# Row variances of an 8192 x 8192 matrix: 64 KiB pieces on one queue, a quarter of each row summed on ScalarE, last row in shrinking pieces

## The chip, the cores and the metric

The kernel runs on one core of a Trainium2 chip. The metric is the time of one execution on the device in microseconds (us), the median of several runs. The profile kept for each kernel is that of one of these executions; its span is about 1.8 us shorter than the time (653.6 against 655.4 us for the kernel before); it is counted from the first instruction of the program. Every run quoted here was at the full granted clock.

## The reference

```python
x = np.random.randn(8192, 8192).astype(np.float32)   # 268.44 MB
out = np.var(x, axis=1)                               # 8192 variances
```

Every element must be loaded once and used once, so there are two candidates for the bound: the loads, and the engine that reduces.

## The kernel before

A tile is 128 rows, one row of 8192 values (32 KiB) per partition. It is loaded as two halves of 2 MiB, one from SyncE's and one from ScalarE's queue; a half is 16 KiB per partition. VectorE computes count, mean and squared deviation of each stretch of 512 columns (`bn_stats`), and one `bn_aggr` joins the 16 stretches of the row. At the end TensorE turns the 64 columns of variances into rows, and one transfer writes them.

```python
data = ctx.enter_context(tc.tile_pool(name="data", bufs=4))
CH = 2; spc = nsub // CH; LOOK = 3                  # nsub = 16
def issue_dma(t):
    xt = data.tile([P, nsub, FMAX], mybir.dt.float32)
    for c in range(CH):
        lo = c * spc; hi = lo + spc
        dma_eng[c % 2].dma_start(out=xt[:, lo:hi, :], in_=x_t[t, :, lo:hi, :])
    ...
def compute(t):
    ...
    for j in range(nsub):
        nc.vector.bn_stats(out=st[:, j, :], in_=xt[:, j, :])
    mv = stats.tile([P, nc.vector.BN_AGGR_DIM], mybir.dt.float32)
    nc.vector.bn_aggr(out=mv, in_=st)
    nc.gpsimd.tensor_copy(out=var_all[:, t : t + 1], in_=mv[:, 1:2])
...
nc.tensor.transpose(vp, var_all, ident)             # after the loop
nc.scalar.copy(vs, vp)
nc.sync.dma_start(out=out_t, in_=vs)
```

## Time and profile before

| | before |
|---|---|
| time, median of 4 runs | 655.37 us (655.24 to 655.69) |
| span of the profiled run | 653.6 us |
| VectorE busy | 636.2 us (97%) |
| pace of the loads in the middle | 428 GB/s |

Loads are carried by 16 transfer engines, piece by piece; such a piece, here 16 KiB, is called a packet below. The page of the kernel before: busy time by engine, the two loading queues with the instruction queue (packets, MB, share of the 16 transfer engines' time), the chain of work that ended last, and VectorE's groups (busy us, mean ns of one, idle before them and what ended it).

```profile
PE 0.4 (0%) x1; PEld 0.1 (0%) x1; DVE 636.2 (97%) x1088; ACT 1.5 (0%) x2; POOL 12.4 (2%) x70
...
q1 hardware_dynamic: 9296, 134.25, 48.4%
q10 hardware_dynamic: 9216, 134.22, 48.2%
q14 instruction: 12, 0.10, 0.0%
...
DVE 88%; DMA 6%; issue 5%; SPq 0%; PE 0%; ACT 0%; POOLq 0%; POOL 0%
...
L61 DVE BATCH_NORM_STATS2 st<-xt 128x6 f32<-128x512 f32 x1024 | 610.1, 673 | 13.6 <-DMA xt<-in_x_dram 13.6
L63 DVE BATCH_NORM_AGGREGATE mv<-st 128x2 f32<-128x96 f32 x64 | 36.4, 570 | 0.1
```

VectorE looks like the bound: it waits 13.6 us in all, nearly all of it for the first tile. But the two loading queues together were also active for 96.6% of the transfer engines' time. The next view tells the two apart. It is the kernel before in chosen stretches of the span (us): length, busy time of each engine with its number of instructions, granted clock, share of the transfer engines' time, GB/s.

```profile
200.00:300.00 100.00, 0.00 (x0) 0.00 (x0) 100.00 (x172) 0.00 (x0) 1.83 (x10) 1.00 1.01 428
620.00:625.00 5.00, 0.00 (x0) 0.00 (x0) 5.00 (x9) 0.00 (x0) 0.18 (x1) 1.00 1.01 429
625.00:630.00 5.00, 0.00 (x0) 0.00 (x0) 5.00 (x10) 0.00 (x0) 0.00 (x0) 1.00 0.80 341
630.00:635.00 5.00, 0.00 (x0) 0.00 (x0) 5.00 (x9) 0.00 (x0) 0.18 (x1) 1.00 0.06 26
635.00:640.00 5.00, 0.00 (x0) 0.00 (x0) 5.00 (x10) 0.00 (x0) 0.00 (x0) 1.00 0.03 13
```

In the middle the transfer engines are never idle (share 1.01) and carry 428 GB/s, a little more than VectorE consumes: its period is 9.934 us per tile of 4.194 MB, 422 GB/s. Both are saturated and almost equally fast. The last lines matter as much: most transfer engines finish at about 630 us, but 26 GB/s remain until 635 and 13 in the stretch after it. 428/16 is 26.8, so this is one engine of the 16, some 8 us late. A tile is complete only when its last engine has delivered, so this engine decides when VectorE may start. The end of VectorE's timeline before (start, length, instructions):

```profile
630.32 9.53 DVE L61 BATCH_NORM_STATS2 st<-xt 128x6 f32<-128x512 f32 x16
639.77 0.57 DVE L63 BATCH_NORM_AGGREGATE mv<-st 128x2 f32<-128x96 f32 x1
640.26 8.93 DVE L61 BATCH_NORM_STATS2 st<-xt 128x6 f32<-128x512 f32 x15
649.29 0.59 DVE L63 BATCH_NORM_AGGREGATE mv<-st 128x2 f32<-128x96 f32 x1
```

The landing records (each transfer engine reports when its part of a load has arrived) show the last tile complete at 638.46 us, 7.8 us after its second latest engine, and VectorE began it at 640.26. Relieving VectorE alone can hardly gain anything.

### The profile page before, as it was taken

Reading aid. Unit: us, or ns where it says so; the run is one execution under the profiler, and the core shown is the slowest. Engines: PE = TensorE matmul, PEld = TensorE weight load, DVE = VectorE, ACT = ScalarE, POOL = GpSimd, SP = SyncE. Lnnn points to the kernel's source line nnn. Section 1 sums busy time; section 2 is a strip of 40 time slices with the busy share of each in tenths; the row PEclk is TensorE's granted clock in tenths of the full one; section 3 lists DMA queues with packets and bytes.
Section 4 is the critical chain, followed back from the end, with each engine's and each line's share of the span. In section 5 each row is a group of like instructions: output and inputs, shape, how many; then the busy total and the mean of one; then the engine's idle time right before and its main releaser. Section 6 shows DMA issues by size and latency. Waiting matters only on the chain.

```text
span 653.6 us, 1512 instructions
## 1 busy us (share of the span) xinstructions
PE 0.4 (0%) x1; PEld 0.1 (0%) x1; DVE 636.2 (97%) x1088; ACT 1.5 (0%) x2; POOL 12.4 (2%) x70
## 2 busy tenths in 40 slices
PE   0000000000000000000000000000000000000000
PEld 0000000000000000000000000000000000000000
DVE  2999999999999999999999999999999999999997
ACT  0000000000000000000000000000000000000000
POOL 0000000000000000000000000000000000000000
DMA  8999999999999999999999999999999999999950
GB/s 369 433 430 425 427 432 428 425 431 428 427 428 430 427 427 430 427 427 428 428 426 431 427 429 427 426 429 428 428 427 430 427 428 429 429 425 430 429 222 2
DMA packets 18524, 268.57 MB, mean 411 GB/s; under 512 B 2064, under 2 KB 2128, under 8 KB 2128
## 3 DMA queue, kind: packets, MB, share of 16 engines
q1 hardware_dynamic: 9296, 134.25, 48.4%
q10 hardware_dynamic: 9216, 134.22, 48.2%
q14 instruction: 12, 0.10, 0.0%
HBM read 268.44 MB, written 0.03 MB: 411 GB/s over the span
## 4 chain that ended last, share of the span: by engine, by line
DVE 88%; DMA 6%; issue 5%; SPq 0%; PE 0%; ACT 0%; POOLq 0%; POOL 0%
DVE st L61 82%; DMA xt<-in_x_dram 6%; DVE mv L63 5%; SPq L54 0%; PE vp L74 0%; ACT vs L76 0%; POOLq L103 0%; POOL var_all L64 0%
## 5 line engine op out<-in xcount | busy, mean ns | idle before, releaser
L61 DVE BATCH_NORM_STATS2 st<-xt 128x6 f32<-128x512 f32 x1024 | 610.1, 673 | 13.6 <-DMA xt<-in_x_dram 13.6
L63 DVE BATCH_NORM_AGGREGATE mv<-st 128x2 f32<-128x96 f32 x64 | 36.4, 570 | 0.1
L64 POOL COPY var_all<-mv 128x1 f32<-128x1 f32 x64 | 11.7, 183 | 637.1 <-DVE mv L63 637.1
L76 ACT ACT_TABLE_LOAD x1 | 1.3, 1283 | 609.9 <-DMA xt<-in_x_dram 609.9
L74 PE MATMUL vp<-ident,var_all 128*64 128x128 f32 x1 | 0.4, 421 | 650.2 <-POOL var_all L64 650.2
L76 ACT COPY vs<-vp 64x128 f32<-64x128 f32 x1 | 0.3, 258 | 39.5 <-PE vp L74 39.5
masks.py:199 POOL TENSOR_SCALAR_AFFINE_SELECT ident<-ident 128x128 f32<-128x128 f32 x1 | 0.3, 292 | 0.1
L74 PEld LDWEIGHTS vp<-ident,var_all 128*64 128x64 f32 x1 | 0.1, 128 | 650.2 <-POOL var_all L64 650.2
masks.py:197 POOL MEMSET ident<- 128x128 f32 x1 | 0.2, 204 | 0.3 <-POOLq L92 0.3
L92 POOL MEMSET const-float32-0.0<- 128x1 f32 x1 | 0.1, 98 | 0.2 <-issue 0.2
L92 POOL MEMSET const-bfloat16-1.0<- 128x1 bf16 x1 | 0.1, 101 | 0.0
L92 POOL MEMSET const-uint8-127<- 128x1 uint8 x1 | 0.1, 101 | 0.0
L92 POOL MEMSET const-float32-1.0<- 128x1 f32 x1 | 0.1, 98 | 0.0
## 6 DMA issues: line engine op xcount, KB each, us to landing
xt<-in_x_dram ACTq DMA_DIRECT2D x64, 2048.0 KB, 29.1
xt<-in_x_dram SPq DMA_DIRECT2D x64, 2048.0 KB, 28.9
out_dram<-vs SPq DMA_DIRECT2D x1, 32.0 KB, 1.8
```

Source lines behind the costliest of these rows:

```text
L61: nc.vector.bn_stats(out=st[:, j, :], in_=xt[:, j, :])
L63: nc.vector.bn_aggr(out=mv, in_=st)
L64: nc.gpsimd.tensor_copy(out=var_all[:, t : t + 1], in_=mv[:, 1:2])
L74: nc.tensor.transpose(vp, var_all, ident)
L76: nc.scalar.copy(vs, vp)
L92: nc = _bacc.Bacc("TRN2", target_bir_lowering=False, num_devices=1)
```

## The change

The intent: take work off VectorE, so that the loads alone bound the kernel; make the loads' pieces larger; and let the last data arrive in shrinking pieces, so that little work is left behind it.

- A tile is now 256 rows: two adjacent rows per partition, 64 KiB contiguous in memory, loaded by one 8 MiB transfer on SyncE's queue, with three buffers. There are 32 tiles.
- VectorE does 12 of the 16 stretches of a row. ScalarE sums the other 2048 columns, shifted by a mean from the first stretch, and sums their squares; GpSimd turns the two sums into one more entry for the aggregate.
- The last tile comes as one row and then 4096, 2048, 1024, 512, 256, 256 columns of the other row, which VectorE does alone. Its variances are written by a transfer of their own.

```diff
-    data = ctx.enter_context(tc.tile_pool(name="data", bufs=4))
+    data = ctx.enter_context(tc.tile_pool(name="data", bufs=3))
...
+    x_t = x.rearrange("(t p j) f -> t p (j f)", p=P, j=J)          # J = 2
...
+    def row_stats(xt, j):
+        for c in range(DC):                                        # DC = 12
+            bn(st, c, xt[:, o + c * F : o + (c + 1) * F])
+        k = st[:, 1:2]
+        src = xt[:, o + DC * F : o + m]
+        nc.scalar.activation(out=junk, in_=src, func=ACTF.Identity, bias=k, scale=-1.0,
+                             accum_out=s12[:, 0:1])
+        nc.scalar.activation(out=junk, in_=src, func=ACTF.Square, bias=k, scale=-1.0,
+                             accum_out=s12[:, 1:2])
+        ... five GpSimd operations on [128, 1]
...
+    for t in range(NT - 1):                                        # NT = 32
+        xt = data.tile([P, J * m], FP32, name="xt")
+        nc.sync.dma_start(out=xt, in_=x_t[t])
+        for j in range(J):
+            st = row_stats(xt, j)
+            pending.append((st, t, j))
+            if len(pending) > 1:
+                finish(*pending.pop(0))
...
+    nc.sync.dma_start(out=xt[:, 0:m], in_=x_t[t, :, 0:m])          # last tile
+    pieces = [4096, 2048, 1024, 512, 256, 256]
+    lo = m
+    for w in pieces:
+        nc.sync.dma_start(out=xt[:, lo : lo + w], in_=x_t[t, :, lo : lo + w])
+        lo += w
...
+        nc.sync.dma_start(out=out_last[t], in_=var_last)           # [128, 2]
```

More of the change, by code (lines that the diff above doesn't have):

```diff
@@ L7 @@
 from concourse._compat import with_exitstack
+FP32 = mybir.dt.float32
+ACTF = mybir.ActivationFunctionType
+ALU = mybir.AluOpType
 @with_exitstack
@@ L19 @@
     n, m = x.shape
-    FMAX = nc.vector.BN_STATS_FMAX
-    assert m % FMAX == 0
-    nsub = m // FMAX
-    assert n % P == 0
-    ntiles = n // P
-    x_t = x.rearrange("(t p) (s f) -> t p s f", p=P, f=FMAX)
-    out_t = out.rearrange("(t p) -> t p", p=P)
-    data = ctx.enter_context(tc.tile_pool(name="data", bufs=4))
-    stats = ctx.enter_context(tc.tile_pool(name="stats", bufs=8))
+    F = nc.vector.BN_STATS_FMAX
+    J = 2
+    NT = n // (P * J)
+    C = m // F
+    AC = 4
+    DC = C - AC
@@ L33 @@
+    NA = AC * F
+    T3 = 3
+    x_t = x.rearrange("(t p j) f -> t p (j f)", p=P, j=J)
+    out_tj = out.rearrange("(t q) -> t q", q=P * J)
+    out_last = out.rearrange("(t p j) -> t p j", p=P, j=J)
+    data = ctx.enter_context(tc.tile_pool(name="data", bufs=3))
+    stats = ctx.enter_context(tc.tile_pool(name="stats", bufs=6))
+    small = ctx.enter_context(tc.tile_pool(name="small", bufs=6))
     singles = ctx.enter_context(tc.tile_pool(name="singles", bufs=1))
     psum = ctx.enter_context(tc.tile_pool(name="psum", bufs=1, space=bass.MemoryType.PSUM))
-    outp = ctx.enter_context(tc.tile_pool(name="outp", bufs=1))
@@ L37 @@
-    var_all = singles.tile([P, ntiles], mybir.dt.float32)
-    ident = singles.tile([P, P], mybir.dt.float32)
-    make_identity(nc, ident)
-    dma_eng = [nc.sync, nc.scalar]
-    CH = 2
-    spc = nsub // CH
-    xts = [None] * ntiles
-    LOOK = 3
-    def issue_dma(t):
-        xt = data.tile([P, nsub, FMAX], mybir.dt.float32)
-        for c in range(CH):
-            lo = c * spc
-            hi = lo + spc
-            dma_eng[c % 2].dma_start(out=xt[:, lo:hi, :], in_=x_t[t, :, lo:hi, :])
-        xts[t] = xt
@@ L57, in compute @@
-    def compute(t):
-        xt = xts[t]
-        st = stats.tile([P, nsub, nc.vector.BN_STATS_DIM], mybir.dt.float32)
-        for j in range(nsub):
-            nc.vector.bn_stats(out=st[:, j, :], in_=xt[:, j, :])
-        mv = stats.tile([P, nc.vector.BN_AGGR_DIM], mybir.dt.float32)
-        nc.vector.bn_aggr(out=mv, in_=st)
-        nc.gpsimd.tensor_copy(out=var_all[:, t : t + 1], in_=mv[:, 1:2])
-    for t in range(ntiles):
-        issue_dma(t)
-        if t >= LOOK:
-            compute(t - LOOK)
@@ L70, with bn @@
-    for t in range(ntiles - LOOK, ntiles):
-        compute(t)
-    vp = psum.tile([ntiles, P], mybir.dt.float32)
-    nc.tensor.transpose(vp, var_all, ident)
-    vs = outp.tile([ntiles, P], mybir.dt.float32)
-    nc.scalar.copy(vs, vp)
-    nc.sync.dma_start(out=out_t, in_=vs)
+    var_all = singles.tile([P, J, NT], FP32)
+    var_last = singles.tile([P, J], FP32)
+    junk = psum.tile([P, NA], FP32)
+    def bn(st, at, src):
+        nc.vector.bn_stats(out=st[:, at * 6 : at * 6 + 6], in_=src)
@@ new lines, in row_stats @@
+    def row_stats(xt, j):
+        st = stats.tile([P, DC * 6 + T3], FP32)
+        s12 = small.tile([P, 2], FP32)
+        tmp = small.tile([P, 2], FP32)
+        o = j * m
+        for c in range(DC):
[6 more added lines that the diff above has]
+                             accum_out=s12[:, 1:2])
+        b = DC * 6
+        nc.gpsimd.memset(st[:, b : b + 1], float(NA))
+        nc.gpsimd.tensor_scalar(out=tmp[:, 0:1], in0=s12[:, 0:1], scalar1=1.0 / NA, scalar2=0.0,
+                                op0=ALU.mult, op1=ALU.add)
+        nc.gpsimd.tensor_tensor(out=st[:, b + 1 : b + 2], in0=k, in1=tmp[:, 0:1], op=ALU.subtract)
+        nc.gpsimd.tensor_tensor(out=tmp[:, 1:2], in0=s12[:, 0:1], in1=tmp[:, 0:1], op=ALU.mult)
+        nc.gpsimd.tensor_tensor(out=st[:, b + 2 : b + 3], in0=s12[:, 1:2], in1=tmp[:, 1:2], op=ALU.subtract)
+        return st
@@ new lines, in finish @@
+    def finish(st, t, j):
+        mv = small.tile([P, 2], FP32)
+        nc.vector.bn_aggr(out=mv, in_=st)
+        nc.gpsimd.tensor_copy(out=var_all[:, j, t : t + 1], in_=mv[:, 1:2])
+    pending = []
+    for t in range(NT - 1):
[6 more added lines that the diff above has]
+                finish(*pending.pop(0))
@@ new lines @@
+    t = NT - 1
+    xt = data.tile([P, J * m], FP32, name="xt")
+    nc.sync.dma_start(out=xt[:, 0:m], in_=x_t[t, :, 0:m])
[4 more added lines that the diff above has]
+        lo += w
+    st = row_stats(xt, 0)
+    finish(*pending.pop(0))
+    ident = singles.tile([P, P], FP32)
+    make_identity(nc, ident)
+    vs = singles.tile([NT - 1, P, J], FP32)
+    for j in range(J):
+        vp = psum.tile([NT - 1, P], FP32, name="vp")
+        nc.tensor.transpose(vp, var_all[:, j, 0 : NT - 1], ident)
+        nc.scalar.copy(vs[:, :, j], vp)
@@ new lines @@
+    nc.sync.dma_start(out=out_tj[0 : NT - 1], in_=vs)
+    stl = stats.tile([P, (C + 1) * 6], FP32, name="stl")
+    lo, i = m, 0
+    while lo < 2 * m:
+        w = F
+        if 2 * m - lo <= 512:
+            w = 256
+        bn(stl, i, xt[:, lo : lo + w])
+        lo += w
+        i += 1
+        if i == 2:
+            mv = small.tile([P, 2], FP32)
+            nc.vector.bn_aggr(out=mv, in_=st)
+            nc.gpsimd.tensor_copy(out=var_last[:, 0:1], in_=mv[:, 1:2])
+    mv = small.tile([P, 2], FP32)
@@ L81 @@
+    nc.vector.bn_aggr(out=mv, in_=stl[:, 0 : i * 6])
+    nc.vector.tensor_copy(out=var_last[:, 1:2], in_=mv[:, 1:2])
+    with nc.allow_non_contiguous_dma(reason="two values per partition"):
+        nc.sync.dma_start(out=out_last[t], in_=var_last)
 _INS = ['x']
```

## The prediction

> **What bounds the kernel now.** VectorE and the loads are almost exactly balanced. The page gives VectorE 636.2 us busy of 653.6 (97%). The timeline repeats a tile every 9.934 us (16 statistics at about 0.59 us start to start, one 0.49 us aggregate): 4.19 MB per 9.934 us is 422 GB/s. In the view by stretches the DMA share is 1.01 at 428 GB/s in every 100 us from 100 to 600: the queues always hold work, so 428 is the transfers' own pace. In that view the loads drop off at about 629 us, but 26 and 13 GB/s remain at 630-635 and 635-640: one of 16 engines (428/16 = 26.8) is some 8 us late. The packet records show why: 12 instruction fetches of 8 KB, each stretching one load packet by 0.35-0.66 us. So the last tile is complete only near 638.7 us, and VectorE starts it at 640.3. Removing VectorE work alone can therefore gain little: loads bound the rest.
>
> **What the change does.**
> - VectorE: 12 of 16 statistics per row remain, 12 x 0.59 + 0.49 = 7.57 us a row, 15.1 us per 8.39 MB tile, against 19.4-19.6 us of loading. VectorE no longer bounds the middle; it idles about 4.4 us per tile.
> - ScalarE: two activations of 2048 columns per row. No such instruction is in the trace; the Trainium skill, "ScalarE: Activation LUTs", What ACT_TABLE_LOAD costs, gives 280 + 0.833 N ns with a pointer bias: estimate 2.0 us each, 4 us a row. GpSimd: five small operations at about 0.18 us (the duration of its copies). Both hide under VectorE's row.
> - Loads: packets of 64 KiB instead of 16 KiB. Packets of 8 KB took 0.309 us and of 16 KB 0.611 us, so 8 KB more costs 0.302 us; estimate for 64 KiB 0.611 + 6 x 0.302 = 2.42 us, 433 GB/s. The skill's "DMA: Bandwidth & Descriptors", Where 436 GB/s comes from, puts the ceiling at 435; the 428 here is consistent. Gain over all loads: about 7.5 us. Refilling a buffer 15 us after it lands leaves more than a tile queued, so one queue and three buffers suffice.
> - Instruction fetches: about as many (fewer for VectorE, more for GpSimd and ScalarE); one engine stays about 7.5 us late.
>
> **The end decides.** A whole tile is now 64 KiB per partition, so VectorE begins the next to last tile only when all of it is in. At that moment it owes 24 + 12 + 17 statistics and 4 aggregates: 14.7 + 7.6 + 10.8 = 33.1 us, while the last tile's data needs only 20 us. The shrinking pieces find VectorE about 13 us behind; they save nothing.
>
> Sum: start of data 2.8 us; 31 tiles x 8 packets x 2.424 = 601.2; late engine 7.5; landing 0.4: tile 31 of 32 ready near 612. VectorE 33.1: 645. Output 2.7 as now (650.9 to 653.6): span 647.7. Time less span is now 1.8: **649 us**, range 642 to 656. Faster by over 2%: 0.15; within 2%: 0.81; slower: 0.04.
>
> **What would show it.** Packets of 64 KiB near 2.42 us and 431-434 GB/s in the middle; VectorE waiting for each load, some 4 us a tile; ScalarE about 40% busy; VectorE without a wait from the landing of the next to last tile (near 612) to its last aggregate, about 33 us; no wait on the small pieces; a chain of waits that is mostly DMA, then VectorE; one engine landing 7-8 us after the others.
>
> **What would make it wrong.** 64 KiB packets split, or no faster: then about 656. Pauses between packets on a single queue, or memory slower for this pattern: slower still. The late engine catching up, or fewer fetches: about 642. GpSimd's chain slower than VectorE's row: aggregates wait.

## The result

The changed kernel takes **648.66 us** (648.52 to 648.95, 4 runs) against 655.37. The ratio is 0.9897, 95% interval 0.9883 to 0.9911: 1% faster. Ratios in this document are the mean time of one kernel's runs over that of the kernel before in the same rounds, so they are not quite the ratio of the medians. The result is correct, as in every run below.

The page of the changed kernel: busy time, queues, the chain that ended last, and the largest groups.

```profile
PE 0.8 (0%) x2; PEld 0.3 (0%) x2; DVE 485.3 (75%) x838; ACT 265.5 (41%) x255; POOL 58.9 (9%) x384
...
q1 hardware_dynamic: 5648, 268.47, 96.2%
q14 instruction: 15, 0.12, 0.1%
...
DMA 72%; DVE 26%; issue 1%; SPq 0%; DVEq 0%
...
L50 DVE BATCH_NORM_STATS2 st<-xt 128x6 f32<-128x512 f32 x756 | 451.6, 678 | 157.2 <-DMA xt<-in_x_dram 157.2
L63 ACT ACTIVATE junk<-xt,st 128x2048 f32<-128x2048 f32 x63 | 124.2, 1971 | 339.4 <-DVE st L50 339.4
```

VectorE is relieved of 151 us (636.2 to 485.3), yet the time fell by 6.7. Its waits for loads rose from 13.6 to 157.2 us instead, and the chain that ended last is now 72% loading, where it was 88% VectorE. The changed kernel in stretches, the same columns as before:

```profile
200.00:300.00 100.00, 0.00 (x0) 0.00 (x0) 77.69 (x135) 44.14 (x43) 9.76 (x63) 1.00 1.00 433
620.00:625.00 5.00, 0.30 (x1) 0.12 (x1) 5.00 (x10) 1.81 (x2) 0.70 (x4) 1.00 0.54 203
625.00:630.00 5.00, 0.12 (x1) 0.00 (x0) 5.00 (x9) 4.23 (x5) 0.71 (x4) 1.00 0.05 18
630.00:635.00 5.00, 0.42 (x1) 0.13 (x1) 5.00 (x10) 0.26 (x1) 0.37 (x2) 1.00 0.02 4
635.00:640.00 5.00, 0.00 (x0) 0.00 (x0) 5.00 (x10) 0.00 (x0) 0.00 (x0) 1.00 0.01 2
```

The loads run at 433 GB/s instead of 428 in this stretch and are practically over by 630 us; after that VectorE is almost alone. (The view counts a packet whole at its start. Sixteen packets of 64 KiB are 1.05 MB, so a stretch of 100 us can read some GB/s too high or too low: the five from 100 to 600 us read 430, 433, 435, 431 and 434. With each packet spread over its own duration they read 433.1 to 433.5, and 427.9 to 428.2 in the kernel before.) The end of VectorE's timeline in the changed kernel:

```profile
609.66 14.34 DVE L50 BATCH_NORM_STATS2 st<-xt 128x6 f32<-128x512 f32 x24 [4.26 <-DMA xt<-in_x_dram]
623.91 0.48 DVE L78 BATCH_NORM_AGGREGATE mv<-st 128x2 f32<-128x75 f32 x1
624.31 7.16 DVE L50 BATCH_NORM_STATS2 st<-xt 128x6 f32<-128x512 f32 x12
631.37 0.48 DVE L78 BATCH_NORM_AGGREGATE mv<-st 128x2 f32<-128x75 f32 x1
631.77 1.23 DVE L50 BATCH_NORM_STATS2 stl<-xt 128x6 f32<-128x512 f32 x2
632.90 0.48 DVE L124 BATCH_NORM_AGGREGATE mv<-st 128x2 f32<-128x75 f32 x1
633.30 8.41 DVE L50 BATCH_NORM_STATS2 stl<-xt 128x6 f32<-128x512 f32 x15
641.74 0.62 DVE L127 BATCH_NORM_AGGREGATE mv<-stl 128x2 f32<-128x102 f32 x1
```

The bracket in the first line is its last wait: 4.26 us for tile 31 of 32. From 609.66 us on VectorE works without a gap. Although the last pieces shrink to 256 columns, no statistic on them (`stl`) waits for anything: they had all arrived while VectorE was still on earlier rows.

### The profile page after: what moved, and what is told of

Read it like the earlier page. It is cut to its first block, busy times and chain, and to the rows that moved or that the text cites. A ratio compares the mean times of both kernels' runs of the same rounds, so it can differ in the third digit from the quotient of the medians.

```text
span 646.7 us, 1908 instructions
## 1 busy us (share of the span) xinstructions
PE 0.8 (0%) x2; PEld 0.3 (0%) x2; DVE 485.3 (75%) x838; ACT 265.5 (41%) x255; POOL 58.9 (9%) x384
## 4 chain that ended last, share of the span: by engine, by line
DMA 72%; DVE 26%; issue 1%; SPq 0%; DVEq 0%
DMA xt<-in_x_dram 72%; DVE st L50 25%; DVE stl L50 1%; DVE mv L127 0%; DVE mv L78 0%; DVE mv L124 0%; SPq L84 0%; DVEq L50 0%; DVE var_last L128 0%
## 5 line engine op out<-in xcount | busy, mean ns | idle before, releaser
L50 DVE BATCH_NORM_STATS2 st<-xt 128x6 f32<-128x512 f32 x756 | 451.6, 678 | 157.2 <-DMA xt<-in_x_dram 157.2
L63 ACT ACTIVATE junk<-xt,st 128x2048 f32<-128x2048 f32 x63 | 124.2, 1971 | 339.4 <-DVE st L50 339.4
L65 ACT ACTIVATE junk<-xt,st 128x2048 f32<-128x2048 f32 x63 | 124.2, 1971 | 2.0
L69 POOL TENSOR_SCALAR tmp<-s 128x1 f32<-128x1 f32 x63 | 12.0, 190 | 387.9 <-ACT junk L63 387.9
L78 DVE BATCH_NORM_AGGREGATE mv<-st 128x2 f32<-128x75 f32 x62 | 25.8, 457 | 0.0
L73 POOL TENSOR_TENSOR st<-s,tmp 128x1 f32<-128x1 f32 x63 | 11.9, 189 | 100.6 <-ACT junk L65 100.6
L71 POOL TENSOR_TENSOR st<-st,tmp 128x1 f32<-128x1 f32 x63 | 11.9, 189 | 5.2
L72 POOL TENSOR_TENSOR tmp<-s,tmp 128x1 f32<-128x1 f32 x63 | 11.9, 189 | 0.0
L63 ACT ACTIVATION_READ_ACCUMULATOR junk<-xt,st 128x1 f32 x63 | 11.7, 186 | 0.0
L65 ACT ACTIVATION_READ_ACCUMULATOR junk<-xt,st 128x1 f32 x63 | 11.7, 186 | 0.0
L50 DVE BATCH_NORM_STATS2 stl<-xt 128x6 f32<-128x512 f32 (+1 forms) x17 | 9.6, 645 | 0.0
L68 POOL MEMSET st<- 128x1 f32 x63 | 6.2, 98 | 0.3 <-POOLq L145 0.3
L124 DVE BATCH_NORM_AGGREGATE mv<-st 128x2 f32<-128x75 f32 x1 | 0.5, 481 | 0.0
```

Of the source, the lines that this page charges most:

```text
L50: nc.vector.bn_stats(out=st[:, at * 6 : at * 6 + 6], in_=src)
L63: nc.scalar.activation(out=junk, in_=src, func=ACTF.Identity, bias=k, scale=-1.0, accum_out=s12[:, 0:1])
L65: nc.scalar.activation(out=junk, in_=src, func=ACTF.Square, bias=k, scale=-1.0, accum_out=s12[:, 1:2])
L68: nc.gpsimd.memset(st[:, b : b + 1], float(NA))
L69: nc.gpsimd.tensor_scalar(out=tmp[:, 0:1], in0=s12[:, 0:1], scalar1=1.0 / NA, scalar2=0.0, op0=ALU.mult, op1=ALU.add)
L71: nc.gpsimd.tensor_tensor(out=st[:, b + 1 : b + 2], in0=k, in1=tmp[:, 0:1], op=ALU.subtract)
```

## The experiments

### pad16: packets of 16 KiB, nothing else

```diff
+    x_q = x.rearrange("(t p j) (h f) -> t p (j h) f", p=P, j=J, h=2)
+        xt4 = data.tile([P, 4, m // 2 + 64], FP32, name="xt")
-        nc.sync.dma_start(out=xt, in_=x_t[t])
+        nc.sync.dma_start(out=xt4[:, :, 0 : m // 2], in_=x_q[t])
```

The 64 columns of padding break the destination into four stretches, so one transfer still brings 8 MiB but in packets a quarter as large.

> The changed kernel, but each 64 KiB of a partition lands as four stretches of 16 KiB with a small gap between them, so one transfer of 8 MiB has packets of 16 KiB (0.61 us each) and nothing else differs. Theory (the packet size sets the pace): a tile takes 32 x 0.6125 = 19.60 us instead of 19.36, so 31 tiles cost 7.5 us more: about 656 us, 428 GB/s in the middle. Rival (the pace rose because of one queue or fewer transfers): 648.7 us and 433 GB/s.

Measured: 656.16 us, ratio 1.0012 (0.9999 to 1.0024). The packet records show 16 KiB packets of 0.615 us at the median, where the changed kernel's 64 KiB packets take 2.420. Four small ones would take 2.460 by these durations, though successive packets overlap a little. The stretches of pad16:

```profile
200.00:300.00 100.00, 0.00 (x0) 0.00 (x0) 75.41 (x130) 41.89 (x40) 9.23 (x60) 1.00 1.01 428
```

One queue, three buffers and one transfer per tile do not change the pace; the packet size does. It is worth 7.5 us here (656.16 against 648.66, each beside a kernel before of 655.4), all of the changed kernel's gain.

### dve16: the larger pieces without the offload

```diff
-        for c in range(DC):
+        for c in range(C):                 # all 16 on VectorE; ScalarE and GpSimd sums removed
```

> The changed kernel with all 16 statistics of a row on VectorE; ScalarE and GpSimd sum nothing. Theory (without the offload VectorE bounds again, now starting a whole 8 MiB tile late): 22.7 + 63 x 9.93 + 10.9 + 4.1 = 663 us span, about 665 us, no waits of VectorE in the middle. Rival (the loads alone decide and the offload is idle decoration): 649 us.

Measured: 665.36 us, ratio 1.0152 (1.0139 to 1.0166). In the list of waits VectorE waited for one load only, the first, 22.5 us; before, the first wait was 12.9 us, because the first tile was half as large. So VectorE started 9.6 us later, never waited again, and ended about as much later. Faster packets are worth nothing to an engine that is full; the offload is what lets them count.

### offload: the sums on ScalarE and GpSimd, put into the kernel before

```diff
-        for j in range(nsub):
-            nc.vector.bn_stats(out=st[:, j, :], in_=xt[:, j, :])
+        for j in range(DC):                # DC = 12
+            nc.vector.bn_stats(out=st[:, j * 6 : j * 6 + 6], in_=xt[:, j, :])
+        ... the two activations and five GpSimd operations of the changed kernel
```

> The kernel before with the ScalarE and GpSimd sums alone: 16 KiB packets, two queues, four buffers, transposed output. Theory (packets of 16 KiB keep 428 GB/s, the last tile lands near 637 to 638.7 us, then one row's statistics, 7.2, aggregate, transpose and output, 4.5): about 651 us. Rival (the offload is the whole gain): 648.7 us; rival (the offload alone gains nothing): 655.4 us.

Measured: 653.17 us, ratio 0.9968 (0.9955 to 0.9980). The offload alone gains 2.1 us of the 6.7. I had expected 651; the 2.2 us of difference stand in the list of waits, where VectorE's last two aggregates wait about 1.1 us each for GpSimd. ScalarE had read its last sum by 641.6 us; in GpSimd's timeline each row's small operations come after the copy of the aggregate before, which VectorE finished only at 644.5, so the last three aggregates and GpSimd's operations take turns. The last half tile had been taken up at 636.5 us, a little earlier than expected.

### more_dve: extra VectorE instructions, a test that failed

```diff
+            if t < NT - 2:
+                for _ in range(13):
+                    nc.vector.memset(nop, 0.0)
```

The question was what makes one transfer engine late. The packet records of the changed kernel give a hint. The engines' instructions are fetched as packets of 8 KB on a queue of their own (q14 above), and each of the 14 fetches before tile 31 landed is followed by one long load packet: 3.08 us after six (2.99 after a seventh), 2.76 to 2.80 after the other seven, where the median is 2.42.

> The changed kernel with 13 tiny VectorE fills of one column after each row of the first 30 tiles, 780 more instructions, about 2 us per tile against 4.3 us that VectorE waits there. Theory (instruction fetches slow one transfer engine by about 1 us each, and that engine sets when a tile is complete): 6 more fetches, tile 31 ready some 6 us later: about 654.5 us. Rival (idle time of VectorE costs nothing): 648.7 us.

Measured: 661.62 us, ratio 1.0093 (1.0079 to 1.0107), much more than expected, and for another reason. Nothing tied the fills to their rows, so they were scheduled early: 168 ahead of the first tile, then 66 or 67 per tile until about 250 us. A tile so burdened took 23.3 us instead of 19.4, the buffers came free too late, and the loads fell to 410 GB/s between 100 and 200 us and to 389 between 200 and 300 (the transfer engines' share to 0.95 and 0.92). The run says nothing about fetches. The next two repair it.

### more_dve2 and more_pool2: the extra instructions, tied to their rows

```diff
         nc.gpsimd.tensor_copy(out=var_all[:, j, t : t + 1], in_=mv[:, 1:2])
+        if t < NT - 2:
+            for _ in range(11):
+                nc.vector.tensor_copy(out=nop, in_=mv[:, 0:1])     # more_pool2: nc.gpsimd
```

> The changed kernel with 11 tiny VectorE copies after each row's aggregate in the first 30 tiles, 660 more instructions, tied to the row's result so that they stay in the 4.3 us per tile that VectorE waits (in more_dve they had been gathered ahead and starved the loads). Theory (each instruction fetch of VectorE delays one transfer engine by about 1 us, and that engine says when a tile is complete): 5 more fetches, about 653.7 us, landing spread of tile 31 near 12 us instead of 6.9. Rival (idle time costs nothing): 648.7 us.

> The same 660 extra copies on GpSimd instead of VectorE. Theory (GpSimd's fetches run on another transfer engine, which was 2.7 us behind the fastest where the slowest was 6.9): 5 more fetches bring it to about 6, still not the last: 648 to 649.5 us. Rival (any fetch delays the loads alike): about 653.7 us.

Measured: more_dve2 653.57 us, ratio 0.9977 (0.9964 to 0.9989); more_pool2 648.87 us, ratio 0.9902 (0.9887 to 0.9917). Each has five more fetches than the changed kernel: the page counts 20 packets on the instruction queue in both, against 15. The loads' pace in the middle is unchanged (430 to 436 GB/s in more_dve2 by the view, 432.9 to 433.3 with packets spread over their durations). The VectorE timeline of more_dve2 where tile 31 arrives:

```profile
610.08 4.06 DVE L83 COPY nop<-mv 128x1 f32<-128x1 f32 x22
614.40 14.34 DVE L51 BATCH_NORM_STATS2 st<-xt 128x6 f32<-128x512 f32 x24 [0.26 <-DMA xt<-in_x_dram]
```

And of more_pool2:

```profile
609.75 14.34 DVE L51 BATCH_NORM_STATS2 st<-xt 128x6 f32<-128x512 f32 x24 [4.28 <-DMA xt<-in_x_dram]
```

In more_dve2 VectorE had finished the extra copies and still had to wait for the load, so the load itself came 4.7 us later (614.40 against 609.66), and the time rose by 4.9. The trace records when each of the 16 transfer engines reports its part of a tile. For tile 31, the latest and the second latest engine came after the earliest by:

| kernel | latest | second latest | load packets of 2.98 to 3.08 us behind a fetch, before that landing | of 2.71 to 2.80 us | time |
|---|---|---|---|---|---|
| changed | 6.90 us | 2.73 us | 7 | 7 | 648.66 us |
| more_dve2 | 11.8 us | 2.8 us | 12 | 7 | 653.57 us |
| more_pool2 | 7.1 us | 6.1 us | 7 | 12 | 648.87 us |

The trace does not name the transfer engine of a packet, but landings and packets together fit one reading: VectorE's fetches run on the engine that is latest anyway, about 1 us for each; GpSimd's run on another one, which they bring from 2.7 to 6.1 us, still not the latest. The packets add up to the same: a VectorE fetch of about 0.32 us and the 0.66 us by which the load packet behind it is longer make 0.98; seven of these are about 6.9 us and twelve 11.8, as the latest engine lags. So 660 instructions in idle time of VectorE cost 4.9 us, and as many on GpSimd nothing that can be told from noise. That the fetches make the late engine late is shown by these two runs. Why a fetch of 0.31 to 0.33 us also stretches a load packet by up to 0.66 us is not shown.

### bufs2: two buffers

```diff
-    data = ctx.enter_context(tc.tile_pool(name="data", bufs=3))
+    data = ctx.enter_context(tc.tile_pool(name="data", bufs=2))
```

> The changed kernel with two buffers instead of three. Theory (a buffer is free 14.7 us after its tile landed, 4.6 us before the next tile is in, more than the 2 to 3 us that a first load takes to start; the fastest transfer engines run up to 6.9 us ahead and will pause, the slowest not): within 1 us of 648.7, at most 650. Rival (the queue must hold more than a tile at all times): each of 30 tiles loses some us, 660 or more.

Measured: 649.48 us, ratio 0.9910 (0.9896 to 0.9923), whose interval overlaps that of the changed kernel. The pace is 429.3 GB/s instead of 433.2 (100 to 600 us, packets spread over their durations), and the latest engine is only 3.0 us behind the earliest at tile 31: the earliest reports it 4.7 us later than in the changed kernel (607.33 against 602.66), the latest 0.8 (610.38 against 609.57). So the fast ones give up their lead, as expected, but not by pauses between packets: the 64 KiB packets took 2.441 us in the mean instead of 2.425, about 4 us over the 248 of each engine. Why they are longer is not shown. The third buffer buys less than a microsecond.

### tail: the last two tiles in pieces

```diff
-        nc.sync.dma_start(out=xt, in_=x_t[t])
+        if t < NT - 2:
+            nc.sync.dma_start(out=xt, in_=x_t[t])
+        else:
+            for lo in range(0, J * m, 2048):
+                nc.sync.dma_start(out=xt[:, lo : lo + 2048], in_=x_t[t, :, lo : lo + 2048])
...
-    pieces = [4096, 2048, 1024, 512, 256, 256]
-    lo = m
+    pieces = [2048] * 7 + [1024, 512, 256, 256]
+    lo = 0
```

> The changed kernel with the last two tiles loaded in pieces of 2048 columns (the last 2048 still as 1024, 512, 256, 256), nothing else. Theory (VectorE owes 33 us of work when tile 31 of 32 lands, against 20 us of loading left): it can now start on the parts, keeps up, and ends about 1 us after the last data at 629.5: about 637.5 us, range 636 to 640. Rival (the end is set by the late engine and the output write): 648 to 649 us.

Measured: 645.00 us, ratio 0.9842 (0.9828 to 0.9855). It gains 3.7 us, not 11. VectorE's timeline in this run:

```profile
590.39 14.34 DVE L50 BATCH_NORM_STATS2 st<-xt 128x6 f32<-128x512 f32 x24 [5.26 <-DMA xt<-in_x_dram]
604.64 0.48 DVE L78 BATCH_NORM_AGGREGATE mv<-st 128x2 f32<-128x75 f32 x1
...
628.95 8.41 DVE L50 BATCH_NORM_STATS2 stl<-xt 128x6 f32<-128x512 f32 x15
637.39 0.62 DVE L130 BATCH_NORM_AGGREGATE mv<-stl 128x2 f32<-128x102 f32 x1
```

The last wait is now for tile 30, which is still a whole tile. It owes 15.1 us when it lands, and VectorE catches up by only 4.3 us per tile (19.4 of loading less 15.1 of work). My estimate had left that debt out. The mechanism was right, but the pieces have to begin several tiles earlier.

### best3: rows for three tiles, then pieces

```diff
+        if t < NT - 4:
+            nc.sync.dma_start(out=xt, in_=x_t[t])
+        else:                               # three tiles in two rows each
+            for j in range(J):
+                nc.sync.dma_start(out=xt[:, j * m : (j + 1) * m], in_=x_t[t, :, j * m : (j + 1) * m])
...
+    pieces = [2048] * 6 + [1024] * 3 + [512, 256, 256]        # the whole last tile
...
+    # last row: ScalarE sums columns 2048 to 4095, VectorE the other 6144
-    AC = 4
+    AC = 5                                  # stretches of a row on ScalarE
```

> A version against the backlog at the end: the last three tiles before the last are loaded as two rows of 32 KiB per partition each, the last tile in pieces of 2048 and fewer columns, ScalarE takes 5 of 16 stretches of a row instead of 4, and also 2048 columns of the very last row. Theory (the run tail moved the backlog to the tile before instead of removing it; with 15.1 us of work per tile against 19.4 of loading it takes several tiles in rows to catch up): VectorE ends about 2 us after the last data at about 629, time 636 to 639. Rival (the end is limited by something other than VectorE's backlog): 645, as tail.

Measured: 638.38 us, ratio 0.9745 (0.9732 to 0.9758). VectorE's timeline at the end of best3:

```profile
609.62 13.15 DVE L50 BATCH_NORM_STATS2 st<-xt 128x6 f32<-128x512 f32 x22 [2.57 <-DMA xt<-in_x_dram]
622.68 0.45 DVE L77 BATCH_NORM_AGGREGATE mv<-st 128x2 f32<-128x69 f32 x1
623.05 2.40 DVE L50 BATCH_NORM_STATS2 stl<-xt 128x6 f32<-128x512 f32 x4
626.93 0.47 DVE L130 BATCH_NORM_AGGREGATE mv<-st 128x2 f32<-128x69 f32 x1 [1.48 <-POOL st L65]
627.32 4.84 DVE L50 BATCH_NORM_STATS2 stl<-xt 128x6 f32<-128x512 f32 x9
632.26 0.52 DVE L133 BATCH_NORM_AGGREGATE mv<-stl 128x2 f32<-128x81 f32 x1
```

VectorE waits again for the data of the last tile, at 609.6, and its final aggregate starts at 632.3 us instead of 641.7. Several things differ from the changed kernel here, but all act on what VectorE owes at the end: the middle still runs on 64 KiB packets, and the latest transfer engine is still 7.0 us behind. With the debt the late end has gone, 10.3 us of it, so the backlog was its reason; the shares of the smaller transfers and of ScalarE's larger part were not measured apart. A wait of 1.48 us for GpSimd is left.

### best_out: the last variances written as one piece

```diff
-    nc.vector.tensor_copy(out=var_last[:, 1:2], in_=mv[:, 1:2])
-        nc.sync.dma_start(out=out_last[t], in_=var_last)
+    nc.tensor.transpose(vp[0:1, :], mv[:, 1:2], ident)
+    nc.vector.tensor_copy(out=vs_last[:, :, 1], in_=vp[0:1, :])
+    nc.sync.dma_start(out=out_tj[t : t + 1], in_=vs_last)
```

> The kernel of best3 with the last tile's variances turned by TensorE into one row and written as one piece of 1 KiB, instead of 128 pieces of 8 bytes. In the changed kernel the write of 8-byte pieces took 4.1 us from its issue to the end of the span, the before kernel's write of 512-byte rows 2.7. Theory (the small pieces cost that difference): the write takes 2.7 or less, the turning adds about 0.8, so about 0.5 us is gained: 637.8. Rival (the write takes as long whatever its pieces): 639.2.

Measured: 637.29 us, ratio 0.9725 (0.9712 to 0.9738). The two ratios overlap a little, but the timelines speak for themselves. In best3 the write is issued at 633.03 and the span ends at 637.5, 4.5 us later. In best_out:

```profile
632.28 0.52 DVE L135 BATCH_NORM_AGGREGATE mv<-stl 128x2 f32<-128x81 f32 x1 [0.55 <-POOL stl L65]
632.95 0.37 PE L137 MATMUL vp<-ident,mv 128*1 128x128 f32 x1 [5.45 <-DVE mv L135]
633.36 0.28 DVE L138 COPY vs_last<-vp 1x128 f32<-1x128 f32 x1 [0.56 <-PE vp L137]
633.71 0.25 SPq L139 DMA_DIRECT2D out_dram<-vs_last  x1
```

The final aggregate starts at the same time (632.28 against 632.26), the turning puts the issue off by 0.68 us, and the span ends at 635.7, 2.0 us after the issue. In these two executions writing 128 pieces of 8 bytes cost 2.5 us more than writing one of 1 KiB. The profiled run of best3 was its slowest (639.3 us); the medians differ by 1.1 us, which with the 0.68 us of turning makes 1.8. In all nine profiled runs that write 8-byte pieces, the time from the issue to the end of the span lies between 4.1 and 4.9 us. It is not the moving that takes it: in best3 the 128 packets took 7 to 9 ns each and were over at 634.08, and the last report of landing came at 636.68. What happens between is not shown. This is the fastest version, 2.8% faster than the kernel before and 1.7% faster than the changed one by the ratios.

## Why the prediction was right

The prediction said 649 us, within 642 to 656, and 648.66 was measured. Point by point:

- **Both limits nearly equal before: right.** offload takes a quarter of VectorE's statistics out of the kernel before and gains 2.1 us; dve16 gives it faster loads and, through the larger first tile, loses 10. Only both together gain more than that.
- **64 KiB packets near 2.42 us: right.** 2.420 at the median; 433.1 to 433.5 GB/s in the middle, packets spread over their durations, against 431 to 434 predicted. pad16 gives back 7.5 us, the predicted amount. The Trainium skill, "DMA: Bandwidth & Descriptors", Where 436 GB/s comes from, gives 435 as the ceiling of the fabric, and the 433 here agree with it; the same section names about 358 as what binds a load from memory (one core's half of a shared memory), which the one core here exceeded. Single stretches of other runs read up to 439 in the view; that is its way of counting (the 439 of more_dve are 433.5 with packets spread).
- **ScalarE and GpSimd hidden: right.** The skill's formula ("ScalarE: Activation LUTs", What ACT_TABLE_LOAD costs) gave 1.99 us, the trace has 1.971. What it did not give is a separate read of the accumulator, 186 ns after each. ScalarE was 41% busy.
- **One late engine, through instruction fetches: right**, 6.9 us at tile 31 against 7.5 predicted; the cause is shown by more_dve2 and more_pool2.
- **VectorE works 33.1 us without a wait from the landing of tile 31: right**, 609.66 to 642.54 is 32.9. It was about 13 us behind the last data, as predicted (the last load ended at 629.2 by its landing record, VectorE at 642.5). That the shrinking pieces saved nothing follows from the absence of waits on them.
- **The output 2.7 us: wrong.** It took 4.1 us from issue to the end of the span, because it is now written in 8-byte pieces; best_out shows that the pieces make the difference. A term in the other direction covered it: tile 31 was ready at 609.6, not 612, because the first load packet began at 1.75 us where the sum has 2.8, a tile took 19.36 us and not 19.39, and the late engine was 6.9 and not 7.5 us late. The predicted span was 647.7, the measured one 646.7. So the mechanism was right, and that the time came within 0.4 us is partly luck: errors of 2.4 and 1.4 us stood against each other.

The small gain of a large change has three parts. Of the 151 us taken from VectorE nearly all turned into waits for loads. The larger packets made the loads about 7.5 us faster. And the larger tile set VectorE 13 us behind at the very end, which best3 mostly took back.

## What to carry to other kernels

When two resources are both at 97%, relieving one gains almost nothing until the other is made faster too; check the loads' pace in the middle against the consumer's before moving work. At the end of a stream, add up the work that the consumer owes when the last whole transfer lands and compare it with the loading time still left: small last pieces help only if the consumer has caught up by then, and with a small advantage per tile that takes several tiles in smaller transfers. Instructions issued in an engine's idle time are not free, as more_dve2 showed, if their fetches run on the transfer engine that is already the last.

## What the Trainium skill lacked or had wrong

- "Runtime: NRT & Kernel Launch", Instruction fetch mechanics, speaks of refills in 16 KiB blocks whose cost is "mostly hidden". Here the fetches were packets of 8 KB, and they were not hidden from the loads: a VectorE fetch took 0.32 to 0.33 us and the load packet behind it 3.08 instead of 2.42 us. 660 more VectorE instructions, five fetches, cost 4.9 us; 660 more on GpSimd, whose fetches ran on another transfer engine, 0.2.
- "DMA: Bandwidth & Descriptors", Bandwidth, gives bandwidth by the size of the transfer and treats small descriptors as the problem. It does not say that packets above 16 KiB still gain: 428 GB/s with packets of 16 KiB, 433 with 64 KiB, at the same 8 MiB transfer (pad16).
- The same page, Specifications, sets a minimum of 512 B for line rate but gives no time for tiny writes: 128 pieces of 8 bytes took 4.1 to 4.9 us from issue to the end of the span in nine runs, one piece of 1 KiB 2.0 (best_out).
- "ScalarE: Activation LUTs" names an accumulator output but not its cost: a separate instruction of 186 ns after each activation here.
